# Hybrid encoder block: the start addresses of the matmul operand tiles in SBUF

## The chip, the cores and the metric

The kernel runs on one core of one Trainium2 chip. The metric is the device time of one execution in microseconds (us); less is better. The median of two runs before the change is 2856.68 us (2855.43 to 2857.94).

## The reference

One layer of an encoder block on a sequence of 2048 tokens with 1024 features, in float32. Shortened to what is computed:

```python
h = rms_norm(x, mix_norm)
z = h @ w_in                                   # 1024 -> 3104 columns
cb, cc, cu, q, k, v, g, lr_f, lr_b = split_cols(z)
y_conv = grouped_rms_norm(cb * dwconv3(cc * cu))        # 512 channels
o = gla(q, k, v, log_a_f) + flipped_gla(q, k, v, log_a_b) - diag   # 4 heads, chunks
y_gla = rms_norm(o) * silu(g)
x = x + concat([y_conv, y_gla]) @ w_out
x = x + softmax(rms_norm(x) w_xq · (rms_norm(mem) w_xk)^T / 16) (rms_norm(mem) w_xv) @ w_xo
x = x + square(relu(rms_norm(x) @ w_up)) @ w_down      # 1024 -> 4096 -> 1024
return rms_norm(x, final_norm)
```

The memory `mem` has 256 rows, the cross-attention 4 heads of 256 features.

## The kernel before, in words

Activations are held with features on the 128 partitions and tokens along the free dimension. A block is 512 tokens (`TB`), a weight matrix is read in pieces of 128 x 1024.

**Products in three terms.** Each float32 operand of the large products is split by `split` (lines 109 to 111) into a high part, rounded to the float32r format by ScalarE, and a low part, the difference, made by VectorE. `mm3` (lines 136 to 140) then forms three matmuls that accumulate in PSUM: high x high (L138), high x low (L139) and low x high (L140). The first operand in the code is the stationary one (the weights of the array, 128 x 128), the second the moving one. Each matmul instruction in the trace has a load of its stationary operand beside it (PEld), also where two matmuls in a row use the same one.

**The stages, in order.** The memory side of the cross-attention (`kv_mm`, `xa_key`, `xa_value`), folded into two matrices in DRAM; for each half of the sequence the in-projection: `qk` and `conv` (through `mtiles`, lines 209 to 218: weights stationary, 512 tokens moving) and `lr_g` and `vg` (through `token_major`, lines 231 to 237: tokens stationary, 288 or 256 columns of weights moving); the gated linear attention (lines 367 to 509); the output projection (lines 871 to 903, 512 tokens moving); the cross-attention in 8 steps of 256 tokens (`xa_scores` with 512 columns of keys moving, `xa_out` with 256 tokens moving); and the MLP (lines 962 to 1047): for each half of the sequence 16 groups of two pieces of `w_up` and `w_down`, with 512 columns moving in nearly all products.

**Where operands lie.** All working tiles are in the pool `big`. Each tag has a fixed number of buffers that its tiles take in turn, and the tags lie one behind the other in the order of their first use: t2, g, gt, raw, a, sm, st, cv, gs. The helpers that hand out tiles are lines 41 to 66:

- `A4`: tag a, 25 buffers of 1024 elements (4096 bytes a partition): weights and normalised activations, high and low
- `G4`: tag g, 8 buffers of 1024 elements; `GT`: tag gt, 8 buffers of 512; `T2`: tag t2, 7 buffers of 512: further operands, activations on their way, results
- `ST`: tag st, 2 buffers of 2048 elements: weights (`load_st`, line 129, and every second piece in `vg_load`, lines 250 to 253), the states of the scan, y of block 2 (line 578), the last two pieces of the scores' keys, the first four accumulators of the MLP
- `RAW`: tag raw, 3 buffers of 1024 elements, where weights land before they are split; `CV`: tag cv, 3 buffers of 1028 elements
- `SM`: tag sm, 11 buffers of 16 elements; `GS`: tag gs, 9 buffers of 16

Elements have 4 bytes. Before the tags come 16,384 bytes of scratch for DMA descriptors and the constants; the first buffer of t2 is at byte 20,608, which is 161 x 128. Buffers of a, g, gt and t2 thus all begin at a multiple of 128 bytes. The sm tiles take 11 x 64 = 704 bytes in front of st, so the st tiles begin at 64 mod 128. The slices that the matmuls take (512 or 1024 or 2048 bytes apart, 1152 for the pieces of 288 columns) keep that place.

**What sets the order.** Instructions of an engine run in the order that a scheduler gives them; in the stretches under `manual_schedule` TensorE's order (and in one of them ScalarE's and VectorE's) is the order of the code. Transfers are issued by SyncE. A tile that is asked for waits until an earlier tile of its tag is let go.

Of the kernel before, what the change touches and what calls it, by code (L numbers as in the profile page):

```python
# [17 lines left out]
P = 128  # L18
# [5 lines left out]
NMEM = 256  # L24
# [6 lines left out]
def block_kernel(ctx, tc, x, mem, wm, wv, wlg, wlog, wout, wxk, wxv, wxqT, wxo, wup, wdn,  # L31
                 vecs, ones, consts, out):
    nc = tc.nc
# [5 lines left out]
    NA, NG = 25, 8  # L39

    def A4(dt=F32, shape=(P, 1024)):
        return big.tile(list(shape), dt, tag="a", name="a4", bufs=NA)

    def G4(dt=F32, shape=(P, 1024)):
        return big.tile(list(shape), dt, tag="g", name="g4", bufs=NG)

    def ST(dt=F32, shape=(P, 2048)):
        return big.tile(list(shape), dt, tag="st", name="st", bufs=2)

# [6 lines left out]
    def T2(dt=F32, shape=(P, 512)):  # L56
        return big.tile(list(shape), dt, tag="t2", name="t2", bufs=7)

    def GT(dt=F32, shape=(P, 512)):
        return big.tile(list(shape), dt, tag="gt", name="gt", bufs=8)  # L60

# [11 lines left out]

    # ---- constants
    cst = cpool.tile([P, 514], F32, name="cst")
# [16 lines left out]

    # ---- scratch in DRAM
    zq = [dram.tile([P, S], F32, name=f"zq{i}") for i in range(2)]
# [20 lines left out]
    def behind(*keys):  # L115
        """what follows is queued behind the last load or split of weights"""
        st = ExitStack()
        for k in keys:
            st.enter_context(tc.issue_after(mark[k].ins))
        return st  # L120
# [28 lines left out]
    def rstd_col(sq, PT):  # L149
        """sums of squares over the features, left on each partition -> 1 / rms, tokens on partitions"""  # L150
        m = sq.shape[-1] // P
        ps = PT()
        for i in range(m):
            nc.tensor.matmul(ps[:, i:i + 1], sq[:, i * P:(i + 1) * P], onec, start=True, stop=True)
        return rstd_of(ps[:, :m], m, D, eng=nc.vector)

    def to_rows(rc, PT):
        """one value per token, tokens on partitions -> the same on all partitions"""
        m = rc.shape[-1]
        r = PT()[:, :m * P]  # L160
        for i in range(m):
            nc.tensor.matmul(r[:, i * P:(i + 1) * P], rc[:, i:i + 1].broadcast_to([P, P]), ident,  # L162
                             start=True, stop=True)
        return r
# [7 lines left out]
    def fold(tiles, SQ, eng):  # L172
        """squares of the tiles [P, 2, n], summed up"""
        acc = None
        for t in tiles:
            sq = SQ()
            nc.scalar.activation(sq, t, AF.Square)
            if acc is None:
                acc = sq
            else:  # L180
                eng.tensor_tensor(out=acc, in0=acc, in1=sq, op=ALU.add)
        eng.tensor_tensor(out=acc[:, 0], in0=acc[:, 0], in1=acc[:, 1], op=ALU.add)
        return acc[:, 0]
# [10 lines left out]
    def prep_step(res, gain, r, kp, xt):  # L194
        """two feature tiles of a block of 512 tokens, normalised: hi and lo [P, 2 kt, 512]"""
        hi, lo = A2(F32R), A2(F32R)
        for j in range(2):
            kt = 2 * kp + j
            nc.vector.scalar_tensor_tensor(out=xt[:, j], in0=xt[:, j], scalar=gain[:, kt:kt + 1], in1=r,  # L199
                                           op0=ALU.mult, op1=ALU.mult)  # L200
        split(xt, hi, lo)
        res.append((hi, lo))

    # =========================== in-projection ===========================
    save = cpool.tile([P, 4, 8], F32, name="save")
# [3 lines left out]
    def mtiles(tiles, blks, ws=None):  # L209
        """tiles: (index, evac); the whole group for one block, then for the other one"""  # L210
        ws = ws or [load_w(wm[idx]) for idx, _ in tiles]
        for bi, blk in enumerate(blks):
            for w, (_, evac) in zip(ws, tiles):
                ps = PS()
                for kt in range(KT):
                    sl = slice(kt * P, (kt + 1) * P)
                    mm3(ps, (w[0][:, sl], w[1][:, sl]), blk_op(blk, kt), kt == 0, kt == KT - 1)
                evac(bi, ps)
# [36 lines left out]
    def vg(hf, blks, nxt, meanwhile=None):  # L255
        """columns of v and of silu(g), 256 at a time"""
        for i, (z, c) in enumerate(VG):
            w, nxt = nxt, vg_load(i + 1) if i + 1 < len(VG) else None
            for t in range(8):
                ps = token_major(w, blks, t, 256)  # L260
                vg_store(hf, t, ps, z, c, AF.Copy if z is zv else AF.Silu)
                if meanwhile:
                    next(meanwhile, None)

    def lr_g(hf, blks):
        """low-rank gate inputs (rows f at 0..15, ones at 16, b at 32..47, b one token late) and g's first columns"""
        lr.append((A4(F32R, (64, 1024)), A4(F32R, (64, 1024))))
# [31 lines left out]
    def conv(hf, blks, cs, ws=None, meanwhile=None):  # L299
        # y = B * dwconv3(C * u), channels on partitions  # L300
        n0 = 1022 if hf == 0 else 1026
# [3 lines left out]
        def group(c, ws):  # L305
# [16 lines left out]
            def taps():  # L322
                # T[i] is the convolution at token (t0 + i) in the first half, (t0 - 2 + i) in the second
                nc.vector.tensor_scalar_mul(T[:, :n0], HP[:, 0:n0], cw[:, 3 * c:3 * c + 1])
                for tap in (1, 2):
                    nc.vector.scalar_tensor_tensor(out=T[:, :n0], in0=HP[:, tap:tap + n0],
                                                   scalar=cw[:, 3 * c + tap:3 * c + tap + 1],
                                                   in1=T[:, :n0], op0=ALU.mult, op1=ALU.add)
                if hf == 0:
                    nc.vector.tensor_copy(save[:, c, 0:3], HP[:, 1022:1025])  # L330
                else:
                    nc.vector.tensor_tensor(out=T[:, 0:2], in0=T[:, 0:2], in1=save[:, c, 4:6], op=ALU.mult)
# [32 lines left out]

    # =========================== gated linear attention ===========================
    def gla_decay(h, res):
        """decayed k and q, rows 0..63 for the forward scan and 64..127 for the backward one; in stages"""
        pr, r0 = h // 2, (h % 2) * 64
# [3 lines left out]
        res.append((Q, K, de))  # L373
        # log_sigmoid(z) = min(z, 0) - ln(1 + exp(-|z|))
        for hf in range(2):
# [13 lines left out]
        def sums(hf):  # L389
            nc.vector.tensor_tensor(out=K[hf], in0=Q[hf], in1=K[hf], op=ALU.subtract)  # L390
            for i in range(4):
                sl = slice(i * 256, (i + 1) * 256)
                nc.vector.tensor_tensor_scan(out=Q[hf][:, sl], data0=reset, data1=K[hf][:, sl], initial=0.0,
                                             op0=ALU.mult, op1=ALU.add)
            # sums run from token 0 and from token 64 of a chunk; both become distances to token 63
            pv = Q[hf].rearrange("p (c t) -> p c t", t=P)
# [26 lines left out]
        yield  # L423
        # decay from one chunk's middle to the next one's
        nc.vector.memset(de, 0.0)
# [13 lines left out]
    def gla_states(h, Q, K, de):  # L439
        """steps that leave the state before chunk c in slot c of St"""  # L440
        St = ST(F32, (P, 16, P))
# [68 lines left out]

    # =========================== memory side of the cross-attention ===========================
    rmem = cpool.tile([P, NMEM], F32, name="rmem")
# [18 lines left out]
    def kv_mm(wsrc, h, T, ws=None):  # L531
        """two feature tiles of head h, [P, 2, NMEM]"""
        ps = PS((P, 2, NMEM))
# [52 lines left out]
    def rsqrt(vs, rs):  # L586
        """rs[i] = 1 / sqrt(vs[i]): a first guess and one Newton step"""
        lns = [nc.scalar.activation(r, v, AF.Ln) for v, r in zip(vs, rs)]
# [24 lines left out]
    def y_split(b, kp, y, sqs):  # L613
        """y *= gain / rms over each group of 64 channels (the convolution's); hi and lo"""
        PT = PS if b == 0 else PG
# [18 lines left out]

    # =========================== cross-attention ===========================
    SB = 256
# [232 lines left out]

    # =========================== output projection ===========================  # L870
    nxt += [y_split(0, kp, *y_load(0, kp)) for kp in (2, 3)]
    wo += [load_w(wout[kt]) for kt in range(3, KT)]
    for b in range(4):
        bs = slice(b * TB, (b + 1) * TB)
        yb, nxt = nxt, []
        if b == 3:
            # the weights are let go one after the other
            xts, pss = [], []
# [72 lines left out]

    # =========================== MLP ===========================
    def final_norm(acc, cs, n, hf, sq):
# [10 lines left out]
    for hf in range(2):  # L964
# [11 lines left out]
        for g in range(NG_):  # L976
# [3 lines left out]
            if hf == 0 and g in (NG_ - 4, NG_ - 3):  # L980
                # the next half's 1 / rms
                b = 2 + g - (NG_ - 4)
                r = CV()[:, :TB]
                early.append((r, fold([load_T(x2d, b, kp, RAW((P, 2, TB))) for kp in range(4)], A2, nc.gpsimd)))
# [123 lines left out]
```

## Time and profile before

| | |
|---|---|
| median of 2 runs | 2856.68 us |
| profiled execution, span from first to last instruction | 2856.6 us |
| mean granted TensorE clock | 0.983 |
| instructions | 34,634 |
| matmuls, loads of stationary operands | 14,232 each |
| ACT casts a<-raw of 128x1024 (L110) | 208, 1049 ns each |
| DVE subtractions a<-raw of 128x1024 (L111) | 208, 1245 ns each |
| moved by DMA | 259.92 MB, mean 91 GB/s |

How to read the profile: PE is TensorE's matmuls, PEld its loads of the stationary operand (they run beside a matmul), DVE VectorE, ACT ScalarE, POOL GpSimd, SP SyncE. L138 is line 138 of the kernel; where a helper such as `mm3` issues an instruction, the line is the helper's. `ps<-st,a` names the output, the moving operand and the stationary one by tag, without buffer numbers. In a timeline the columns are start and duration in us. In a table of windows each engine's busy time in the window is followed by the count of its instructions that touch it, then come the granted clock, the share of DMA and GB/s. In a list of groups the numbers behind the bar are busy time in us, mean ns of one instruction, and the idle time of the engine ahead of them with what ended it. A row of waits gives us in total, times, and the longest; a row of DMA issues the count, the size and the us from issue to landing. Matmuls overlap: the duration of one record holds its way through the array, and the distance from one start to the next is what it takes of TensorE's time.

### The profile page before, as it was taken

What the parts mean: (1) busy time and instruction counts of PE and PEld (TensorE: products, weight loads), DVE (VectorE), ACT (ScalarE), POOL (GpSimd) and SP (SyncE); (2) the same over time, 40 slices, a digit from 0 to 9 for tenths busy, and PEclk for the clock granted to TensorE, in tenths of its full rate; (3) what the DMA queues carried; (4) which work ended last, traced back from release to release, by engine and by line L of the source; (5) the groups of instructions that cost most, each with busy time, mean ns of one, the idle gap of its engine ahead of it and who ended that gap; (6) DMA issues with size and microseconds to landing.
All of it is one profiled execution on the core that took longest, in us unless ns stands there. A gap on an engine that the chain in (4) does not pass through costs nothing.

```text
span 2856.6 us, 34634 instructions
## 1 busy us (share of the span) xinstructions
PE 2756.2 (96%) x14232; PEld 2352.7 (82%) x14232; DVE 1413.6 (49%) x2177; ACT 811.6 (28%) x1222; POOL 183.9 (6%) x149
## 2 busy tenths in 40 slices
PE   7999989988989999999999999999999999999997
PEld 6898878877777889999988888888878888888886
DVE  6413372556766544343554544444575454444444
ACT  5411162423445433221321121122232122112122
POOL 1000010302200000000200000002030000000003
PEclk9999999998999999999999999999999999999999
DMA  7412363234445441101621111122153111112111
GB/s 239 157 62 67 109 221 115 88 92 116 129 125 186 144 157 45 60 31 59 214 74 45 45 59 45 45 60 88 60 162 104 45 45 59 45 45 59 45 37 60
DMA packets 140383, 259.92 MB, mean 91 GB/s; under 512 B 12672, under 2 KB 69120, under 8 KB 140224
## 3 DMA queue, kind: packets, MB, share of 16 engines
q1 hardware_dynamic: 140224, 257.70, 28.8%
q8 instruction: 111, 1.82, 0.3%
q14 instruction: 48, 0.39, 0.0%
HBM read 203.13 MB, written 54.53 MB: 90 GB/s over the span
## 4 chain that ended last, share of the span: by engine, by line
PE 64%; issue 2%; DVE 2%; ACT 1%; POOL 1%; DMA 1%; SPq 0%; POOLq 0%; DVEq 0%; ACTq 0%
PE ps L138 11%; PE ps L139 11%; PE ps L140 11%; PE pg L140 10%; PE pg L138 10%; PE pg L139 10%; POOL gt L1039 0%; PE pg L698 0%; DMA raw<-zy 0%; DVE a L111 0%; POOL sm L146 0%; DVE raw L199 0%; PE ps L162 0%; DMA raw<-in_wout 0%; ACT L590 0%
## 5 line engine op out<-in xcount | busy, mean ns | idle before, releaser
L138 PE MATMUL ps<-a,a 128*128 128x512 f32 (+1 forms) x1864 | 706.3, 379 | 7.4 <-DVE t L242 6.7
L139 PE MATMUL ps<-a,a 128*128 128x512 f32 (+1 forms) x1864 | 705.6, 379 | 0.0
L140 PE MATMUL ps<-a,a 128*128 128x512 f32 (+1 forms) x1864 | 704.1, 378 | 0.0
L110 ACT CAST a<-raw 128x1024 fp32r<-128x1024 f32 (+1 forms) x216 | 219.5, 1033 | 702.1 <-PE pg L140 508.1
L138 PEld LDWEIGHTS ps<-a,a 128*128 128x128 f32 x1864 | 354.6, 190 | 74.1 <-DVE t L242 6.2
L111 DVE TENSOR_TENSOR a<-raw,a 128x1024 fp32r<-128x1024 f32 (+1 forms) x216 | 263.5, 1225 | 291.2 <-PE ps L139 205.6
L139 PEld LDWEIGHTS ps<-a,a 128*128 128x128 f32 x1864 | 355.0, 190 | 63.1 <-issue 0.2
L140 PEld LDWEIGHTS ps<-a,a 128*128 128x128 f32 x1864 | 354.7, 190 | 63.4 <-issue 0.4
L138 PE MATMUL pg<-gt,a 128*128 128x512 f32 (+1 forms) x880 | 302.8, 344 | 0.0
L140 PE MATMUL pg<-gt,a 128*128 128x512 f32 (+1 forms) x880 | 302.8, 344 | 0.0
L139 PE MATMUL pg<-gt,a 128*128 128x512 f32 (+1 forms) x880 | 302.7, 344 | 0.0
L1029 DVE TENSOR_TENSOR g<-pg,g 128x512 f32<-128x512 f32 (+1 forms) x260 | 177.3, 683 | 148.0 <-PE pg L140 147.9
L1029 DVE TENSOR_TENSOR st<-pg,st 128x512 f32<-128x512 f32 (+1 forms) x260 | 176.7, 681 | 118.5 <-PE pg L140 118.4
L138 PE MATMUL pg<-g,a 128*128 128x512 f32 (+1 forms) x552 | 213.8, 387 | 3.1 <-DVE st L1029 2.8
L139 PE MATMUL pg<-g,a 128*128 128x512 f32 (+1 forms) x552 | 213.4, 387 | 0.0
L140 PE MATMUL pg<-g,a 128*128 128x512 f32 (+1 forms) x552 | 213.3, 386 | 0.0
L994 ACT ACTIVATE t<-ps 128x512 f32<-128x512 f32 x128 | 76.6, 599 | 424.6 <-PE ps L140 424.6
L996 DVE SCALAR_TENSOR_TENSOR t<-ps,t 128x512 f32<-128x512 f32 x128 | 88.1, 688 | 204.2 <-ACT t L994 204.2
L138 PEld LDWEIGHTS pg<-gt,a 128*128 128x128 f32 x880 | 166.9, 190 | 20.2 <-DVE gt L111 0.3
L139 PEld LDWEIGHTS pg<-gt,a 128*128 128x128 f32 x880 | 167.0, 190 | 19.9
L140 PEld LDWEIGHTS pg<-gt,a 128*128 128x128 f32 x880 | 167.1, 190 | 19.6
L138 PEld LDWEIGHTS pg<-g,a 128*128 128x128 f32 x552 | 103.8, 188 | 24.6 <-DVE st L1029 3.1
(284 smaller groups left out, 3755.3 us busy)
## 6 DMA issues: line engine op xcount, KB each, us to landing
raw<-in_wup SPq DMA_DIRECT2D x64, 512.0 KB, 3.6
raw<-in_wdn SPq DMA_DIRECT2D x64, 512.0 KB, 3.9
raw<-in_wm SPq DMA_DIRECT2D x32, 512.0 KB, 4.1
raw<-x2d SPq DMA_DIRECT2D x48, 256.0 KB, 3.8
a<-in_x SPq DMA_DIRECT2D x32, 256.0 KB, 6.4
gt<-zv SPq DMA_DIRECT2D x32, 256.0 KB, 3.4
raw<-zy SPq DMA_DIRECT2D x32, 256.0 KB, 4.0
raw<-in_wv SPq DMA_DIRECT2D x12, 512.0 KB, 4.6
```

The lines of the kernel that those rows point to most:

```text
L110: mark["act"] = nc.scalar.copy(hi, src)
L111: nc.vector.tensor_tensor(out=lo, in0=src, in1=hi.bitcast(F32), op=ALU.subtract)
L138: nc.tensor.matmul(ps, lh, rh, start=first, stop=False)
L139: nc.tensor.matmul(ps, lh, rl, start=False, stop=False)
L140: mark["pe"] = nc.tensor.matmul(ps, ll, rh, start=False, stop=last)
L994: nc.scalar.activation(r, ps, AF.Relu)
L996: nc.vector.scalar_tensor_tensor(out=u, in0=ps, scalar=0.0, in1=r, op0=ALU.max, op1=ALU.mult)
L1029: nc.vector.tensor_tensor(out=acc[d][:, cs], in0=ps, in1=acc[d][:, cs], op=ALU.add)
```

## The change

The helpers of the tags a, g, st, t2 and gt get their tiles from a new function `flat`. It asks for a tile that is 8 elements (32 bytes) longer, in one dimension, and gives out a view of it that begins at element 0 or at element 4 (16 bytes), by a counter over all calls: three calls with 4, three with 0, and so on. The view has the shape that was asked for. With the longer buffers, neighbouring buffers of one tag begin 32 bytes further on, mod 128. The scratch for DMA descriptors is set to 1024 bytes, which makes the room. All comments and docstrings are removed, so that the line numbers shift by some 15. RAW, CV, SM, GS and PSUM tiles are asked for as before.

```diff
+    count = [0]
+
+    def flat(n, dt, shape, tag, name, bufs):
+
+        t = big.tile([P, n + 8], dt, tag=tag, name=name, bufs=bufs)
+        count[0] += 1
+        o = 4 * (count[0] * 5 // 3 % 2)
+        size = int(np.prod(shape[1:]))
+        t = t[:shape[0], o:o + size]
+        if len(shape) == 3:
+            t = t.rearrange("p (a b) -> p a b", a=shape[1])
+        elif len(shape) == 4:
+            t = t.rearrange("p (a b c) -> p a b c", a=shape[1], b=shape[2])
+        return t
+
     def A4(dt=F32, shape=(P, 1024)):
-        return big.tile(list(shape), dt, tag="a", name="a4", bufs=NA)
+        return flat(1024, dt, shape, "a", "a4", NA)
 
     def G4(dt=F32, shape=(P, 1024)):
-        return big.tile(list(shape), dt, tag="g", name="g4", bufs=NG)
+        return flat(1024, dt, shape, "g", "g4", NG)
 
     def ST(dt=F32, shape=(P, 2048)):
-        return big.tile(list(shape), dt, tag="st", name="st", bufs=2)
+        return flat(2048, dt, shape, "st", "st", 2)
...
     def T2(dt=F32, shape=(P, 512)):
-        return big.tile(list(shape), dt, tag="t2", name="t2", bufs=7)
+        return flat(512, dt, shape, "t2", "t2", 7)
 
     def GT(dt=F32, shape=(P, 512)):
-        return big.tile(list(shape), dt, tag="gt", name="gt", bufs=8)
+        return flat(512, dt, shape, "gt", "gt", 8)
...
-    nc = bacc.Bacc("TRN2", target_bir_lowering=False, num_devices=1)
+    nc = bacc.Bacc("TRN2", target_bir_lowering=False, num_devices=1, dynamic_dma_scratch_size=1024)
```

## The prediction

> **What bounds the kernel now.** I read the page first: busy shares, granted clock, chain, DMA queues.
>
> ```profile
> PE 2756.2 (96%) x14232; PEld 2352.7 (82%) x14232; DVE 1413.6 (49%) x2177; ACT 811.6 (28%) x1222; POOL 183.9 (6%) x149
> PEclk9999999998999999999999999999999999999999
> PE 64%; issue 2%; DVE 2%; ACT 1%; POOL 1%; DMA 1%; SPq 0%; POOLq 0%; DVEq 0%; ACTq 0%
> q1 hardware_dynamic: 140224, 257.70, 28.8%
> ```
>
> TensorE is busy for 96% of the span at nearly full clock, and its own steps are 64% of the chain; nothing else on the chain has more than 2%. The waits of PE, longest first, say the same: the top one is
>
> ```profile
> PE ps L138 <- ACT a L110: 10.6, 3, 9.8
> ...
> PE pg L490 <- DMA gt<-zv: 5.2, 3, 2.3
> ```
>
> 10.6 us out of 2856.6, and the only one on a transfer is 5.2. But "busy" doesn't say whether the matmuls run as densely as they could, so next I looked at stretches in which PE never pauses, by windows and by the timeline (start in us, duration in us).
>
> ```profile
> 1750.00:1850.00 100.00, 100.00 (x443) 82.81 (x442) 49.74 (x68) 19.53 (x27) 0.00 (x0) 1.00 0.17 48
> 2200.00:2300.00 100.00, 100.00 (x443) 82.84 (x442) 49.20 (x67) 19.70 (x27) 0.00 (x0) 1.00 0.17 52
> ```
> ```profile
> 1750.09 0.39 PE L138 MATMUL pg<-gt,a 128*128 128x512 f32 x1
> ...
> 1850.05 0.39 PE L138 MATMUL pg<-g,a 128*128 128x512 f32 x1
> ```
>
> Both windows lie in the MLP. Of the 443 matmuls that touch the first, two had begun before it, so 441 start-to-start intervals fill 1850.05 - 1750.09 = 99.96 us: 226.7 ns each, the same again 450 us later, while DVE has half its time free. The 0.39 us of one record is its latency; the interval is what a matmul costs. So the time of this kernel is mostly the number of matmuls times their interval, and the question is what the interval depends on.
>
> **Does the place of a tile matter already?** In the kernel before, tiles of the tags a, g, gt and t2 are whole multiples of 128 bytes apart and begin at 0 mod 128. The tag st comes behind eleven sm tiles of 64 bytes (704 bytes, five and a half times 128), so the st tiles begin at 64 mod 128. That makes three natural experiments. First, line 252 loads the columns of v and g alternately into st and into a, and the same 192 matmuls (8 token tiles x 8 kt x 3) of 256 columns then read them as moving operand, with weights from tag a:
>
> ```profile
> 178.88 0.29 PE L138 MATMUL ps<-st,a 128*128 128x256 f32 x1
> ...
> 200.65 0.28 PE L138 MATMUL ps<-a,a 128*128 128x256 f32 x1
> ...
> 223.68 0.40 PE L138 MATMUL ps<-a,a 128*128 128x512 f32 x1
> ```
>
> (200.65 - 178.88) / 192 = 113.4 ns from st, (223.68 - 200.65) / 192 = 119.9 ns from a. Second, 512 columns with the moving operand in st (y of block 2), 12 matmuls:
>
> ```profile
> 954.40 0.39 PE L138 MATMUL ps<-st,a 128*128 128x512 f32 x1
> ...
> 957.20 0.39 PE L138 MATMUL ps<-gt,a 128*128 128x512 f32 x1
> ```
>
> 2.80 / 12 = 233.3 ns, against 226.7. Third, 512 columns with the weights in st, 10 intervals:
>
> ```profile
> 580.55 0.39 PE L138 MATMUL ps<-a,st 128*128 128x512 f32 x1
> ...
> 582.84 0.39 PE L139 MATMUL ps<-a,st 128*128 128x512 f32 x1
> ```
>
> 2.29 / 10 = 229.0 ns. The place does matter, by a few per cent, and not in one direction. The difference between 512 and 256 columns at one alignment is 226.7 - 119.9 = 106.8 ns, 0.417 ns a column, so 512 columns take 213.5 ns and 256 take 106.7. What is left over, I call the surplus: 13.2 ns with all at 0, 19.8 with moving st at 512 columns, 6.7 with moving st at 256, 15.5 with weights in st. The steady ones sit about 6.6 ns (16 columns' time) apart.
>
> The fourth view is what happens when PE starts again after a break, with everything at 0 mod 128:
>
> ```profile
> 639.67 0.40 PE L138 MATMUL ps<-a,a 128*128 128x512 f32 x1
> 639.90 0.40 PE L139 MATMUL ps<-a,a 128*128 128x512 f32 x1
> 640.14 0.40 PE L140 MATMUL ps<-a,a 128*128 128x512 f32 x1
> ...
> 641.98 0.39 PE L139 MATMUL ps<-a,a 128*128 128x512 f32 x1
> ```
>
> Ten intervals in 2.31 us, 231.0 ns on average, before a long run settles at 226.7. So 226.7 is a state that equal alignments fall into and keep; a disturbed stream pays about 4 ns more. [...]
>
> **The change part by part.** It removes and adds no instruction and no transfer: `flat` only makes each tile 32 bytes longer and views it from byte 0 or 16. Buffer k of a tag then begins 32 k bytes on, mod 128, and the toggle (three tiles on, three off) adds 16, so all eight multiples of 16 occur, and hi, lo and weights of one product stand at different ones.
>
> *Matmuls of 512 columns.* From the code there are 9,344: 3,104 triples (MLP 2,032, in-projection 512, output projection 256, scores 256, values 32, decay 16) times 3, and 32 from lines 619 and 620. Nearly all run at 226.7 now. Of the eight places of the weights relative to the moving operand one is today's, and seven are others. For those I take the mean of the three disturbed values, (233.3 + 229.0 + 231.0) / 3 = 231.1, which gives 7/8 x 231.1 + 1/8 x 226.7 = 230.5: +3.8 ns x 9,344 = +35.5 us. The bounds are the least and the greatest surplus in the rows, 6.7 and 19.8, that is 6.5 ns less or 6.6 more: -61 to +62 us. My value is nearer the upper side because the two other rows for this very width are slower and none is faster.
>
> *Matmuls of 256 columns.* 3,360, of which 384 (line 252's st) are at 113.4 now in the undisturbed half. I take the midpoint of the two rows, 116.7: -3.2 x 2,976 + 3.3 x 384 = -8.2 us. Bounds: all at 113.4, -6.5 x 2,976 = -19 us; all at 126.5, that is with the greatest surplus, +6.6 x 2,976 + 13.1 x 384 = +25 us. The 384 matmuls of 288 columns and the small ones of the scan I leave as they are.
>
> *VectorE and ScalarE on the shifted tiles.* Two pairs of groups, one with st (64 mod 128) beside g (0), one shifted by a single element beside an unshifted one:
>
> ```profile
> L1029 DVE TENSOR_TENSOR g<-pg,g 128x512 f32<-128x512 f32 x252 | 173.9, 691 | 145.1 <-PE pg L140 145.1
> L1029 DVE TENSOR_TENSOR st<-pg,st 128x512 f32<-128x512 f32 x252 | 173.5, 689 | 116.9 <-PE pg L140 116.9
> L326 DVE SCALAR_TENSOR_TENSOR cv<-cv,vec 128x1022 f32<-128x1022 f32 x8 | 10.3, 1283 | 0.1
> L111 DVE TENSOR_TENSOR a<-raw,a 128x1024 fp32r<-128x1024 f32 x208 | 258.4, 1245 | 291.2 <-PE ps L139 205.6 <-ACT a L110 53.5 <-issue 18.0
> ```
>
> 691 and 689 ns, and 1283 for taps 4 or 8 bytes off against 1245: nothing worth a term. I set it at 0; the cover is DVE's 50% and ACT's 80% of free time in the MLP windows. Were every cast and subtraction 3% slower (1283 / 1245), that cover would still hold.
>
> *Transfers.* Loads into st and g take the same time to land, so 64 bytes cost nothing; 16 were never tried.
>
> ```profile
> st<-x2d SPq DMA_DIRECT2D x8, 512.0 KB, 6.9
> g<-x2d SPq DMA_DIRECT2D x8, 512.0 KB, 6.8
> raw<-in_wup SPq DMA_DIRECT2D x64, 512.0 KB, 3.6
> ```
>
> The weights land in raw, which isn't toggled, so the MLP's queue is untouched. Cost 0, covered by a DMA share of 0.17 there; without that cover it would be one landing more per exposed load, and PE's only listed wait on a transfer is 5.2 us in all. The smaller scratch moves every address by 15,360 bytes, 120 x 128, and all traffic but instructions is on the hardware_dynamic queue of the first fence, so it costs 0.
>
> The sum: 2856.6 (span) + 35.5 - 8.2 = 2883.9, **2884 us**. The span equals the median of the two runs, 2856.68, to 0.1 us, so nothing lies around it that would have to be added.
>
> [...]
>
> **The rivals.** *No difference (0.12).* The drifts cancel, or the interval settles at 226.7 in any mix. For it: most stretches after a break do find it again. Against: st never did. Time 2857. [...]
>
> *Faster (0.13).* [...] For it: 113.4 ns in the first experiment. Against: no row for 512 columns lies below 226.7. Price: half of the 512s at a surplus of 6.7, -3.3 x 9,344 = -31 us, and all 256s at 113.4, -19: 2807. It decides as soon as the mean 512 interval is below 226.7 + 8.2 / 9,344 = 227.6.
>
> *Much slower (0.15).* A tile on an odd multiple of 16 costs a step of its own, 6.6 ns over the worst row: 240 for half of the 512s, 230.5 for the rest, 4,672 x (13.3 + 3.8) = +80, and half of the 256s up by 6.6, half at the midpoint: +10 - 5. Time 2942. It passes 2% once the mean 512 interval exceeds 226.7 + (57 + 8) / 9,344 = 233.7. Nothing in the trace speaks for or against it, as no large operand stands on 16. [...]
>
> **How the numbers follow.** My forecast of a mild loss has 0.60, and the point is its 2884. Its own range is 2865 to 2915. For 8 in 10 I reach into the rivals on both sides, half of the faster one and a third of the much slower one: 2825 to 2930. A change of 2% (57 us) is about what a measurement of this kernel tells from none: below 2800 I see 0.03 (the faster rival at its full bound, 2857 - 61 - 19 = 2777), above 2914 there is 0.17 (0.12 of the much slower rival and 0.05 of my own upper end), and 0.80 within.
>
> **What would show it.** Right: the same 14,232 matmuls, no new wait of note, and in the MLP windows of 100 us about 434 starts in place of 441, with intervals that vary from one to the next (0.22 to 0.24 us in the timeline). Groups of 256 columns nearer 117 ns than 120. DVE and ACT groups of equal duration. Wrong: if the MLP still shows an unbroken 226.7, or less; if intervals of 240 ns appear for the toggled tiles only; if the time is lost in PE's waits, on DMA or DVE, and not in the interval.

## The result, and the profile after

The changed kernel takes **2892.39 us** (median of 2 runs, 2891.06 to 2893.71) against 2856.68 us before: a ratio of 1.0126, with a 95% interval of 1.0097 to 1.0156. It is 36 us slower, under 2% but clear of noise; 2884 (+27) was forecast. The profiled spans differ by the same amount, 2891.9 - 2856.6 = 35.3 us.

The page of the kernel after, in the order in which the page of before was read (busy shares, granted clock, chain, queue):

```profile
PE 2793.8 (97%) x14232; PEld 2349.0 (81%) x14232; DVE 1412.6 (49%) x2177; ACT 811.0 (28%) x1222; POOL 183.9 (6%) x149
PEclk9999999999999999999999999999999999999999
PE 64%; DVE 2%; issue 2%; DMA 2%; ACT 1%; POOL 1%; SPq 0%; POOLq 0%; DVEq 0%; ACTq 0%
q1 hardware_dynamic: 140224, 257.70, 28.2%
```

Every engine runs the instructions it ran before. PE alone has more busy time, 2793.8 against 2756.2 us: +37.6, a little more than the span has grown. DVE, ACT, POOL and the queue stand still, and the clock is no lower. The first two rows of the waits of PE, for ScalarE's casts (L125) and for VectorE's subtractions (L126):

```profile
PE ps L153 <- ACT a L125: 11.3, 2, 9.7
PE ps L155 <- DVE g L126: 7.6, 4, 4.3
```

They were 10.6 and 7.8 us before, so no wait holds the 35 us. The two MLP windows (busy us, and in brackets how many instructions touch the window):

```profile
1750.00:1850.00 100.00, 100.00 (x434) 81.11 (x433) 46.47 (x62) 20.76 (x30) 0.00 (x0) 1.00 0.17 48
2200.00:2300.00 100.00, 100.00 (x433) 81.07 (x432) 46.68 (x62) 20.71 (x28) 0.00 (x0) 1.00 0.17 53
```

PE is still never idle there, at full clock (1.00), and yet 434 matmuls touch the window where 443 did. Two of them began earlier, so 432 starts fill it: 231.5 ns each. The timeline inside the first window (start, duration):

```profile
1749.95 0.40 PE L153 MATMUL ps<-a,a 128*128 128x512 f32 x1
1750.19 0.40 PE L154 MATMUL ps<-a,a 128*128 128x512 f32 x1
1750.43 0.40 PE L155 MATMUL ps<-a,a 128*128 128x512 f32 x1
1750.66 0.40 PE L153 MATMUL ps<-a,a 128*128 128x512 f32 x1
...
1753.45 0.39 PE L153 MATMUL ps<-a,a 128*128 128x512 f32 x1
```

From the first to the last row lie 15 intervals, 3.50 / 15 = 233 ns, and they vary from 0.22 to 0.24 us. Now the groups by shape. First three of before (busy us, mean ns of one record), then the same of after:

```profile
L139 PE MATMUL ps<-a,a 128*128 128x512 f32 x1608 | 632.0, 393 | 0.0
L138 PE MATMUL pg<-gt,a 128*128 128x256 f32 x376 | 106.6, 284 | 0.0
L139 PE MATMUL ps<-st,a 128*128 128x256 f32 x128 | 35.3, 276 | 0.0
```
```profile
L154 PE MATMUL ps<-a,a 128*128 128x512 f32 x1608 | 639.6, 398 | 0.0
L153 PE MATMUL pg<-gt,a 128*128 128x256 f32 x376 | 105.7, 282 | 0.0
L154 PE MATMUL ps<-st,a 128*128 128x256 f32 x128 | 36.0, 281 | 0.0
L1044 DVE TENSOR_TENSOR g<-pg,g 128x512 f32<-128x512 f32 x252 | 173.9, 691 | 151.5 <-PE pg L155 151.5
L126 DVE TENSOR_TENSOR a<-raw,a 128x1024 fp32r<-128x1024 f32 x208 | 258.1, 1244 | 303.8 <-PE ps L154 213.7 <-ACT a L125 61.4 <-issue 18.5
```

Each of the 1,608 matmuls of 512 columns has become (639.6 - 632.0) / 1608 = 4.7 ns longer. The 256s from gt are 2 ns shorter, those from st 5 ns longer. VectorE's groups are what they were (691 ns, and 1244 against 1245).

A record's duration is its interval plus a tail of some 163 ns (389 belongs to 226.7, 276 to 113.3). The table therefore takes start-to-start times from the whole trace. "Mean" is over pairs that follow each other without a pause; "sum" is over all, pauses included:

| matmuls | mean before | mean after | sum before | sum after | difference |
|---|---|---|---|---|---|
| 512 columns | 227.2 ns | 231.8 ns | 2189.5 us | 2232.8 us | +43.3 us |
| 256 columns | 119.1 ns | 117.9 ns | 443.6 us | 440.4 us | -3.2 us |
| 288, 128 and 1 column | | | | | -4.4 us |

Together +35.7 us; the last matmul starts 35.6 us later than before. So the whole loss is in the interval of the 512-column matmuls; the others take a little less than before.

### The profile page after: what moved, and what is told of

Read it like the earlier page. It is cut to its first block, busy times and chain, and to the rows that moved or that the text cites. A ratio compares the mean times of both kernels' runs of the same rounds, so it can differ in the third digit from the quotient of the medians.

```text
span 2891.9 us, 34634 instructions
## 1 busy us (share of the span) xinstructions
PE 2793.8 (97%) x14232; PEld 2349.0 (81%) x14232; DVE 1412.6 (49%) x2177; ACT 811.0 (28%) x1222; POOL 183.9 (6%) x149
## 4 chain that ended last, share of the span: by engine, by line
PE 64%; DVE 2%; issue 2%; DMA 2%; ACT 1%; POOL 1%; SPq 0%; POOLq 0%; DVEq 0%; ACTq 0%
PE ps L153 11%; PE ps L154 11%; PE ps L155 11%; PE pg L154 10%; PE pg L153 10%; PE pg L155 10%; DVE a L126 0%; PE pg L713 0%; DMA raw<-zy 0%; POOL gt L1054 0%; DMA raw<-in_wup 0%; DMA x2d<-cv 0%; ACT a L125 0%; DVE raw L214 0%; ACT L605 0%
## 5 line engine op out<-in xcount | busy, mean ns | idle before, releaser
L153 PE MATMUL ps<-a,a 128*128 128x512 f32 (+1 forms) x1864 | 713.6, 383 | 7.0 <-DVE t L257 6.4
L154 PE MATMUL ps<-a,a 128*128 128x512 f32 (+1 forms) x1864 | 712.5, 382 | 0.0
L155 PE MATMUL ps<-a,a 128*128 128x512 f32 (+1 forms) x1864 | 711.4, 382 | 0.0
L125 ACT CAST a<-raw 128x1024 fp32r<-128x1024 f32 (+1 forms) x216 | 218.9, 1030 | 717.6 <-PE pg L155 520.6
L126 DVE TENSOR_TENSOR a<-raw,a 128x1024 fp32r<-128x1024 f32 (+1 forms) x216 | 263.2, 1224 | 303.8 <-PE ps L154 213.7
L153 PE MATMUL pg<-g,a 128*128 128x512 f32 (+1 forms) x552 | 215.6, 391 | 2.2 <-DVE st L1044 1.9
L154 PE MATMUL pg<-g,a 128*128 128x512 f32 (+1 forms) x552 | 216.2, 392 | 0.0
L155 PE MATMUL pg<-g,a 128*128 128x512 f32 (+1 forms) x552 | 215.8, 391 | 0.0
```

The lines of the kernel that those rows point to most:

```text
L125: mark["act"] = nc.scalar.copy(hi, src)
L126: nc.vector.tensor_tensor(out=lo, in0=src, in1=hi.bitcast(F32), op=ALU.subtract)
L153: nc.tensor.matmul(ps, lh, rh, start=first, stop=False)
L154: nc.tensor.matmul(ps, lh, rl, start=False, stop=False)
L155: mark["pe"] = nc.tensor.matmul(ps, ll, rh, start=False, stop=last)
```

## The experiments

**The theories.** A: a stream of matmuls keeps the fast interval only while the places of their operands (mod 128 bytes) stay the same from one to the next; buffers that step by 32 bytes break that. B: what costs is a tile on an odd multiple of 16 bytes. C: as the prediction had it, the place of the weights relative to the moving operand, mod 128, sets the interval. All edits are against the kernel after, where 4 elements are 16 bytes, and "mean" is that of the table.

**Everything at one odd 16.** The tiles step by 128 bytes, and all views begin at byte 16:

```diff
-        t = big.tile([P, n + 8], dt, tag=tag, name=name, bufs=bufs)
+        t = big.tile([P, n + 32], dt, tag=tag, name=name, bufs=bufs)
-        o = 4 * (count[0] * 5 // 3 % 2)
+        o = 4
```

> All tiles of the five tags are longer by a whole 128 bytes and their views all begin at 16 mod 128 (st at 80), with the small scratch: the new function, the new addresses and the odd multiple of 16 stay, the changing combinations go. Theory A (what costs is that the places change from one matmul to the next, so that the stream never settles): back to the time before, 2850 to 2863 us, and the MLP's steady interval is 226.7 ns again. Theory B (an odd multiple of 16 bytes costs by itself): 2885 us or more, intervals of 230 ns or more in the MLP. Theory C (the place of the weights relative to the moving operand sets the cost): 2850 to 2863, as all stand at the same place.

Measured: 2891.99 us, ratio 1.012 (1.0105 to 1.0135); 512 columns 231.8 ns. Every tile of a, g, t2 and gt begins at 16 mod 128 (st at 80), so nearly all places agree mod 128, and yet the loss is complete. A and C, as stated, fall; B's forecast came out.

**Steps of 32 bytes, no odd 16.**

```diff
-        o = 4 * (count[0] * 5 // 3 % 2)
+        o = 0
```

> The changed kernel without the toggle: buffers 32 bytes apart mod 128, all views from element 0, so only even multiples of 16 occur, in changing combinations. Theory A: nearly all of the loss stays, 2883 to 2896 us, mean interval of the 512-column matmuls 230.5 to 232. Theory B: the loss goes, 2850 to 2865. Theory C: a quarter of the pairs stand at the same place, so a quarter of the loss goes: 2880 to 2886.

Measured: 2891.11 us, ratio 1.0118 (1.0098 to 1.0138); 512 columns 232.0 ns. This time A's forecast came out. The odd 16 isn't needed for the loss, so B alone falls too, and C, which had a quarter of it go.

**Steps of 128 bytes, with the toggle.**

```diff
-        t = big.tile([P, n + 8], dt, tag=tag, name=name, bufs=bufs)
+        t = big.tile([P, n + 32], dt, tag=tag, name=name, bufs=bufs)
```

> The toggle alone: buffers a whole 128 bytes apart, views from 0 or 16 mod 128, three on and three off. Theory A: the stream is disturbed less often, but still at most steps between high and low: 2870 to 2892 us. Theory B: about half of the matmuls read from 16: half of the loss, 2870 to 2880. Theory C: half of the pairs differ: 2872 to 2882. The run measures the toggle's share beside the steps of 32.

Measured: 2888.05 us, ratio 1.0111 (1.0096 to 1.0126); 512 columns 231.6 ns. Again the same loss: within A's range, above those of B and C.

**One combination at a time.** A kernel of matmuls alone (the reference's computation is left out): blocks of 48 with the moving operand at a to h (0 to 112 bytes, in steps of 16) and the weights at a to h; "split" moves only the low parts.

```diff
+            m = 4 * (ml if i % 3 == 1 else mh)
+            w = 4 * (wl if i % 3 == 2 else wh) + 128 * (i // 3 % 8)
+            nc.tensor.matmul(ps[:, :n], W[:, w:w + P], M[:, m:m + n], start=i == 0, stop=i == REP - 1)
```

> A kernel that leaves the whole computation out and measures the matmul alone: blocks of 48 matmuls with a weight load each, at one constant combination of places in steps of 16 bytes mod 128 for each block. First 512 columns, then 256, at all 64 combinations of one place for the moving operand and one for the weights; then 512 columns with the high operands at 0 and the low ones at all 64 combinations. Theory A: a constant combination settles at a steady interval whatever the two places are, on a ladder of 6.7 ns (226.7 or 233.3 at 512 columns, 113.3 or 120.0 at 256); the blocks with different places for high and low settle too, in cycles of three, with means between 224 and 234. Theory C: 226.7 only where both places agree, 230 to 234 at the other 56 combinations. If any combination settles at 220.0, a surplus of one step, a kernel faster than both is possible.

Measured: 1818.19 us in all. Six of its groups of 512 columns, two of them with equal even places, two with equal odd ones:

```profile
L43 PE MATMUL nb_mc_wc<-mov,wgt 128*128 128x512 f32 x48 | 11.0, 389 | 0.0
L43 PE MATMUL nb_mg_wg<-mov,wgt 128*128 128x512 f32 x48 | 11.0, 389 | 0.0
L43 PE MATMUL nb_mb_wc<-mov,wgt 128*128 128x512 f32 x48 | 11.0, 388 | 0.0
L43 PE MATMUL nb_mh_wh<-mov,wgt 128*128 128x512 f32 x48 | 11.4, 396 | 0.0
L43 PE MATMUL nb_mf_wf<-mov,wgt 128*128 128x512 f32 x48 | 11.4, 396 | 0.0
L43 PE MATMUL split_md_we<-mov,wgt 128*128 128x512 f32 x48 | 11.4, 397 | 0.0
```

A block that settles at 226.7 ns from start to start shows 388 or 389, one that stays at 233.3 shows 395 to 397; the intervals named here are read from the starts. Equal even places (a, c, e, g) settle at 226.7 and equal odd ones (b, d, f, h) at 233.3: the relative place is the same in all eight, so it can't be all that decides. Nineteen of the 64 constant combinations settle at 226.7; none is faster. So C, which had 226.7 at the eight equal places alone, fails again, and so does A's ladder of 6.7 ns, as others settle in between, at 228.9, 230.0 or 231.7. Most of them have an odd place in them. Where the weights stand 16 bytes further on than the moving operand, all seven combinations do, from ma_wb to mg_wh: an odd place costs where both operands stand on the same one, and not in every company. (Each combination ran once, from one start.) With split places nearly all stay between 229 and 236. At 256 columns, 113.3 ns appears in all four combinations with the weights 64 bytes further on than the moving operand (and in two others), 120.0 at equal even places.

**Where that left it.** In the kernel before, the step from buffer to buffer is 2,048, 4,096 or (st) 8,192 bytes. In the two runs with steps of 128 it is that and 128 more: the buffers agree mod 128, but no longer mod 256. Theory D: the period is **256 bytes**, and what counts is agreement mod 256. By D the padding alone, if it is a multiple of 256, costs nothing.

**Padding of 128, 256, and 256 with the odd 16.** Three kernels, the longer tiles, `flat` and the smaller scratch in all of them:

```diff
-        t = big.tile([P, n + 8], dt, tag=tag, name=name, bufs=bufs)
+        t = big.tile([P, n + 32], dt, tag=tag, name=name, bufs=bufs)
-        o = 4 * (count[0] * 5 // 3 % 2)
+        o = 0
```

> The views begin at 0, but every buffer of the five tags is 128 bytes longer, so neighbouring buffers stand 128 bytes apart mod 256; every place is still a multiple of 128. Theory D (what has to agree from one matmul to the next is the place mod 256 bytes, not mod 128): as slow as the changed kernel, 2882 to 2895 us, mean 512-column interval above 230.5 ns, and the odd multiple of 16 of the run before had no part in its loss. Theory B (the odd multiple of 16 made the loss of the constant-16 kernel): 2850 to 2863 us.

```diff
-        t = big.tile([P, n + 8], dt, tag=tag, name=name, bufs=bufs)
+        t = big.tile([P, n + 64], dt, tag=tag, name=name, bufs=bufs)
-        o = 4 * (count[0] * 5 // 3 % 2)
+        o = 0
```

> As the last, with 256 bytes in place of 128: all buffers agree mod 256 again, though not mod 512 or beyond; longer tiles, the new function and the small scratch all stay. Theory D: back to 2850 to 2863 us, MLP intervals at 226.7. Rival E (the period is 512 bytes or more, or the small scratch itself costs): 2882 us or more.

```diff
-        t = big.tile([P, n + 8], dt, tag=tag, name=name, bufs=bufs)
+        t = big.tile([P, n + 64], dt, tag=tag, name=name, bufs=bufs)
-        o = 4 * (count[0] * 5 // 3 % 2)
+        o = 4
```

> As the last, with all views of the five tags from 16: one constant odd multiple of 16, agreement mod 256. Theory D: 2850 to 2865 us. Theory B: 2870 us or more. The earlier measurement of places had odd places settle at 226.7 or 233.3 by chance of the start, so a part of the loss, up to 2885, could also remain as a second steady state.

Measured beside 2853.84 us of the kernel before:

| kernel | us | ratio (95%) | 512 columns | 256 columns |
|---|---|---|---|---|
| padding 128 bytes | 2884.83 | 1.0106 (1.0091 to 1.0121) | 231.4 ns | 118.1 ns |
| padding 256 bytes | 2854.01 | 0.9995 (0.9986 to 1.0005) | 227.2 ns | 119.1 ns |
| 256 bytes, all at 16 | 2889.39 | 1.0124 (1.0101 to 1.0148) | 231.6 ns | 117.5 ns |

The MLP windows of padding 128, of padding 256, and of 256 with all at 16:

```profile
1750.00:1850.00 100.00, 100.00 (x434) 81.20 (x433) 48.52 (x66) 21.39 (x30) 0.00 (x0) 1.00 0.17 53
```
```profile
1750.00:1850.00 100.00, 100.00 (x443) 82.81 (x442) 48.58 (x66) 17.54 (x24) 0.00 (x0) 1.00 0.13 42
2200.00:2300.00 100.00, 100.00 (x443) 82.81 (x442) 49.56 (x68) 19.26 (x27) 0.00 (x0) 1.00 0.15 48
```
```profile
1750.00:1850.00 100.00, 100.00 (x437) 81.45 (x436) 48.34 (x66) 19.56 (x27) 0.00 (x0) 1.00 0.16 49
2200.00:2300.00 100.00, 100.00 (x430) 80.57 (x429) 45.63 (x61) 20.87 (x29) 0.00 (x0) 1.00 0.14 45
```

With 256 bytes the 443 of before are back, although the longer tiles, `flat` and the small scratch are all there; with 128 bytes less of padding the kernel is 31 us slower. That is D, and the rival that had the period at 512 bytes or more, or the scratch at fault, falls. But the third kernel speaks against D alone: all its places agree mod 256, at an odd multiple of 16, and it has the whole loss. Its two windows hold 435 and 428 starts, 229.9 and 233.6 ns: one execution, the same places, two speeds. So there are two causes, places that differ mod 256 and all operands on the same odd multiple of 16. Each is enough, and they don't add: the kernel after has both and stands at 231.8 ns, the kernel with the 32-byte steps alone at 232.0, this one at 231.6.

**The period, measured by itself.** Matmuls alone again (the computation is left out), blocks of 96, weights and moving operand both at 128 mod 512 at the start; the moving operand in steps of 64 bytes over 1,024 (nb: 512 columns, ns: 256), the low parts in steps of 128 (split), and steps of 32 (half):

```diff
+            run(f"n{'b' if n == 512 else 's'}_m{H[m]}", n, 4 * m, 4 * m, 0, 0)
...
+            run(f"split_m{L[m]}_w{L[w]}", 512, 0, 8 * m, 0, 8 * w)
```

> The matmul alone again (the computation is left out), blocks of 96. 512 and 256 columns with the moving operand moved in steps of 64 bytes over 960 bytes; 512 columns with the low operands moved in steps of 128 bytes over 896, moving and weights each; the same in small for 256 columns; 256 columns with the moving operand in steps of 32 bytes. Theory D: the answers repeat every 256 bytes: low operands at even multiples of 128 give a steady 226.7 (16 of 64 combinations), the others a mean of 229 to 234; at 256 columns 113.3 comes back at 192, 448, 704 and 960 bytes. Rival E: they repeat every 512 bytes or not at all.

Measured: 2347.34 us. From its groups:

```profile
L43 PE MATMUL nb_me<-mov,wgt 128*128 128x512 f32 x96 | 21.9, 389 | 0.0
L43 PE MATMUL nb_mf<-mov,wgt 128*128 128x512 f32 x96 | 22.2, 391 | 0.0
L43 PE MATMUL nb_mg<-mov,wgt 128*128 128x512 f32 x96 | 22.5, 395 | 0.0
L43 PE MATMUL nb_mh<-mov,wgt 128*128 128x512 f32 x96 | 22.6, 394 | 0.0
L43 PE MATMUL nb_mi<-mov,wgt 128*128 128x512 f32 x96 | 21.9, 389 | 0.0
L43 PE MATMUL split_ma_wc<-mov,wgt 128*128 128x512 f32 x96 | 21.9, 389 | 0.0
L43 PE MATMUL split_ma_wb<-mov,wgt 128*128 128x512 f32 x96 | 22.4, 394 | 0.0
L43 PE MATMUL split_mb_wc<-mov,wgt 128*128 128x512 f32 x96 | 22.6, 395 | 0.0
L43 PE MATMUL ns_ma<-mov,wgt 128*128 128x256 f32 x96 | 11.7, 283 | 0.0
L43 PE MATMUL ns_mh<-mov,wgt 128*128 128x256 f32 x96 | 11.1, 276 | 0.0
```

e is 256 bytes, f 320, g 384, h 448, i 512: 226.7, 228.9, 232.5, 233.3 ns, and from 512 the same again (a to d and m to p repeat it too, a with the start of the kernel in it). In "split", b is 128 bytes and c 256: low parts that are 256 bytes off cost nothing (389); low parts that are 128 bytes off cost 2 to 7 ns (228.9 to 233.4). All 16 combinations of multiples of 256 give 226.7, and no other of the 64. The steps of 32 bytes repeat after 256 as well. The period of 256 is shown. For 256 columns the best place is 192 bytes: 113.3 ns, against 120.0 at 0, which is the slowest of the four steps of 64.

**A version by these rules.** Padding 256 and views by use: the operands that only the 256-column matmuls read as moving begin at byte 192, and st at 64, so that it agrees with the rest.

```diff
+        t = big.tile([P, n + 64], dt, tag=tag, name=name, bufs=bufs)
...
+    def ST(dt=F32, shape=(P, 2048), o=16):
...
+            hi, lo = GT(F32R, (P, 2, NMEM), 48), GT(F32R, (P, 2, NMEM), 48)
...
+            L["p"] = [(GT(F32R, (P, 2, SB), 48), GT(F32R, (P, 2, SB), 48)) for _ in range(4)]
```

> Buffers 256 bytes longer, so that all agree mod 256, and the views placed by use: the moving operand of the 256-column products (attention probabilities, memory, keys, columns of v and g: 3,264 matmuls) stands 192 bytes on from the weights mod 256, where the measurement of places gave 113.3 ns, and everything that meets 512 columns stands at the weights' own place, st tiles included (336 matmuls that had 229 to 233 ns). By theory D: 2,880 matmuls of 256 columns gain 6.5 ns each, 19 us, and the st ones 2 us; some of it sits in stretches that wait for something else, so 2833 to 2842 us, a ratio of 0.992 to 0.995. Rival F (what the matmul alone shows doesn't carry over to the kernel, as the places of the next product differ or other engines read the same memory): 2850 to 2858 us.

Measured: 2846.18 us beside 2852.33, ratio **0.9981** (0.9971 to 0.999). It beats both kernels, by 6 us and not by the 10 to 19 expected: the time lies between D's forecast and F's. One group of 256 columns:

```profile
L152 PE MATMUL pg<-gt,a 128*128 128x256 f32 x376 | 105.7, 282 | 0.4 <-DVE gt L125 0.4
```

276 was wanted here, and 284 had been. Over the trace (an execution of 2844.59 us) the 256s come to 116.0 ns and -8.5 us, the 512s to 227.0 and -3.4 us. Two windows of 20 us, both full of 256-column matmuls with the moving operand at 192, show why:

```profile
160.00:180.00 20.00, 20.00 (x179) 20.00 (x178) 2.88 (x3) 4.30 (x8) 0.00 (x0) 1.00 0.31 101
1167.00:1187.00 20.00, 20.00 (x172) 20.00 (x171) 7.85 (x16) 3.98 (x7) 0.00 (x0) 1.00 0.16 54
```

The same time holds 179 matmuls in one and 172 in the other: some of the blocks at 192 bytes run at 113.3 ns, others in a second steady rhythm of 117.8. Had all of the 3,079 intervals at 192 bytes, 115.9 ns on average, been 113.3, another 8 us would have gone.

**Does the moment of the start decide?** Matmuls alone (the computation is left out): blocks of 96 at one constant place, each behind one matmul of 258 to 288 columns in steps of 2, so that they begin at 16 different moments. Theory G: it is the start that picks the rhythm.

```diff
+        nc.tensor.matmul(ps[:, :shift], W[:, 0:P], M[:, 0:shift], start=True, stop=True)
...
+            run(f"{kind}_{H[j]}", n, m, m, w, w, 258 + 2 * j)
```

> [...] 512 and 256 columns with all at one even place, with all at one odd multiple of 16, and with the moving operand 192 bytes on. Theory G (a constant combination can have more than one steady state, and the moment of the start picks one): at 256 columns and 192 bytes some of the 16 starts end at 113.3 and some at 117.8, as in the kernel with placed views; even and equal places end at 226.7 and 120.0 from every start; the odd place ends at 226.7 from some starts and above 230 from others. Rival H (the place alone picks the state, and what differed in the kernel came from other engines): one value for each of the six kinds, 113.3 for the 192 bytes.

Measured: 1653.67 us. From the groups, equal even places (beven), equal odd 16 (bodd), and 256 columns with the moving operand at 192 (splace):

```profile
L44 PE MATMUL beven_c<-mov,wgt 128*128 128x512 f32 x96 | 22.0, 389 | 0.0
L44 PE MATMUL bodd_h<-mov,wgt 128*128 128x512 f32 x96 | 22.6, 396 | 0.0
L44 PE MATMUL bodd_n<-mov,wgt 128*128 128x512 f32 x96 | 22.4, 393 | 0.0
L44 PE MATMUL bodd_k<-mov,wgt 128*128 128x512 f32 x96 | 22.2, 391 | 0.0
L44 PE MATMUL splace_d<-mov,wgt 128*128 128x256 f32 x96 | 11.5, 281 | 0.0
L44 PE MATMUL splace_g<-mov,wgt 128*128 128x256 f32 x96 | 11.1, 276 | 0.0
```

Even places reach 226.7 from all 16 starts. The odd 16 never does: 233.3 from five, 231.1 from seven, 230.0 from four, 231.5 on average, close to the mean of the kernel with everything at 16 (231.6). The place at 192 settles at 113.3 from nine starts and at 117.8 from seven. So the start picks the rhythm at 192, where the missing half of the gain went, and at the odd 16, which fits the two speeds of that kernel's windows; G's clause that odd places would end at 226.7 from some starts failed.

## Why the prediction was right, and where it wasn't

**What bounds the kernel: right.** The loss is matmuls times interval. DVE, ACT, transfers and waits have the values of before, and the kernel with padding 256 (0.9995, 0.9986 to 1.0005) shows that the code, the longer tiles and the scratch cost nothing that can be measured, as the sum had it.

**"226.7 is a state that equal alignments fall into and keep": right in kind.** The disturbed stream leaves it, by 4.6 ns on average. But only equal even places find it again (from all 16 starts); equal odd ones never did. The forecast window of 434 starts was measured as 432, with the varying intervals that were named.

**The 512-column term: mis-sized, +43.3 instead of +35.5 us.** It fell in two places. One in eight was kept at 226.7, for the weights that stand where they stood relative to the moving operand; in the trace after, sorted by that relative place, those matmuls take 231.3 ns, and the seven others 231.4 to 232.4. An equal pair in a stream that doesn't agree gets next to nothing. And the mean of three disturbed rows, 231.1, was 0.7 ns low. These are worth some 5 and 6.5 us; against them stand 4.7, as the mean before was 227.2 and not 226.7. That the mean of the rows came so close is in part luck: 233.3 and 229.0 are the prices of two constant places (192 and 64 bytes, the 233.3 and 228.9 of the steps of 64), not of a stream whose places change.

**The 256-column term: mis-sized, -3.2 instead of -8.2 us.** The mean came to 117.9, not to the midpoint of 116.7: in the mixed stream no 24 intervals in a row average under 116.7. This error and the first go the same way, 7.8 + 5.0 us; the small matmuls, taken as unchanged, gave 4.4 back. That is the 8.4 us between forecast (+27.3) and trace (+35.7).

**"The place of the weights relative to the moving operand", mod 128: wrong.** The period is 256 bytes. The relative place does set the interval of a constant stream (226.7, 228.9, 232.5 and 233.3 ns in the steps of 64), but it isn't enough: equal relative places gave 226.7 at c and 233.3 at b, and in a stream whose places change, the equal pairs took 231.3. What held 226.7 from every start (16 of 16 in the last run) is that all operands of successive matmuls agree, at an even multiple of 16. Counted mod 256, the st of the kernel before stood 192 bytes from the rest and not 64; the first natural experiment, 113.4 ns from st, was the 192-byte place of the last runs. The prediction's price for st in 512 columns, 233.3, is what the steps of 64 give at 192.

**The rivals.** "No difference" needed the interval to settle in any mix; it never does while places change, and the place isn't free: 227.2 against 231.4 ns between paddings of 256 and 128 bytes. "Faster" rested on 113.4 ns carrying over to 512 columns: no combination tried is below 226.7. "Much slower by the odd 16" was half right. All operands on one odd 16 have a price of their own (1.0124 where nothing else differs from a kernel at 0.9995), but some 4.4 ns and not 13, and it isn't added to the other.

**What stays open.** Why 256 bytes, why the same odd 16 and not one 16 bytes off, what in the start picks the rhythm, and why the outer rhythms lie 6.7 ns apart. Why the place costs anything at all is not shown either: no run has matmuls without a load of weights beside each (14,232 of both in the kernel).

## What to carry to other kernels

Where TensorE is busy all the time, compare start-to-start intervals in a window without a pause: "busy" was 100% both at 226.7 and at 231.5 ns. Where most matmuls have 512 columns, let the operand tiles of successive ones agree mod 256 bytes, at an even multiple of 16, and pad only by multiples of 256: a harmless-looking 32 or 128 bytes cost 1.1 to 1.2% here. For 256 columns the same places gave 120.0 ns, the slow end of what was measured. A place that looks better in one block (113.3 ns) has to be tried from several starts before it is counted on.

## What the hardware showed unasked

- The interval of one and the same matmul takes several steady values by place and by start, among them 226.7, 228.9, 230.0, 231.1, 232.5 and 233.3 ns at 512 columns, and 113.3, 117.8 and 120.0 at 256.
- What is best at one width isn't at the other: 192 bytes apart, 512 columns take the slowest value of the steps of 64 (233.3), 256 columns the fastest (113.3).
- Two disturbances that cost 4 to 5 ns each (places that don't agree, 231.4 ns with padding 128 and 232.0 with the 32-byte steps; all on an odd 16, 231.6 with padding 256) cost the same 4.6 ns together: 231.8 in the kernel after, against 227.2 before.
